# A second tile for the decay matrices in the scan of layer 2, paid for with one general tile

## The chip, the core and the metric

The kernel runs on one core of a Trainium2 chip. The time is that of the device, in microseconds (us), as the median of several executions: 2751.73 us over three (2747.14 to 2757.44). One further execution was profiled. All order, wait and idle times below are from that one.

The engines are TensorE (PE, with PEld for its weight loads), VectorE (DVE), ScalarE (ACT), GpSimd (POOL), and SyncE (SP), which issues the DMAs. Each takes its instructions strictly in the order in which they stand in its queue.

## What is computed

Two model blocks over 1024 tokens of width 1024, all in float32. The change lies in the second layer of the first block, a state-space layer (SSD): an input projection, a short convolution, a scan over chunks of 128 tokens, a gate with a norm, and an output projection. The scan, cut to what matters:

```
cs    = cumsum(dt * a_neg)                         # inside each chunk of 128
decay = where(causal, exp(cs[l] - cs[s]), 0)       # 128 x 128 per head and chunk
cb    = einsum('bclgn,bcsgn->bcgls', cc, bc)       # C times B, per group
y_diag = einsum('bcghls,bcsghp->bclghp', cb * decay, xf)
states = einsum('bclgn,bclghp->bcghpn', bc, xf * decay_states)
h      = h * chunk_decay + states                  # from chunk to chunk
y_off  = einsum('bclgn,bcghpn->bclghp', cc, prev) * exp(cs)
```

There are 32 heads of width 64 in 4 groups (8 heads share one B and C), and 8 chunks.

## The kernel before, in words

Every large product is made of three float32r products (helper `mm3`, lines 189, 193 and 194): each operand is split into a high part (a cast on ScalarE) and a low part (`lo`, line 260, a subtraction on VectorE or GpSimd).

The scan is in `phase_b`. It goes in 32 steps (u, cpair): u counts half groups (4 heads each), cpair pairs of chunks. Eight steps belong to one group. A step has two halves:

- `stage1` transposes x on TensorE (line 891, tile `t`), scales it on VectorE to `Xf` (L898), splits that into `Xh` (L902) and `Xl`; loads `L`, the cumulative sums of 4 heads and 2 chunks spread over 128 partitions, by DMA (L907); makes the decay of it on ScalarE (eight short L911, one exp L913), multiplies it by the masked C-B product `cbm` (L916), and splits it into `Lh` (L918) and `Ll` (L260). Then it adds to the running state: products `t<-Xh,bth`, `hs` on VectorE (L934 to L937), `hh` on ScalarE (L940), `hl`.
- `stage2` makes the output of the step: products of the state (`ch`, `hh`) and of the decay (`Lh`, `Xh`) into the PSUM tiles `u` and `w`, gathered in `et` on VectorE (L971, L974, L988), the gate `zt` (L991), a square on ScalarE (L997), and stores.

```
L = self.tag("L", "L")
nc.sync.dma_start(L..., csd[...].partition_broadcast(128))
...
Lh, Ll = R("Lh"), R("Ll")
nc.scalar.copy(Lh, L)
self.lo(nc.vector, Ll, L, Lh)
```

Beside the scan run the input projections of the groups still to come (PSUM tile `g`, two of them; 48 products of 128x512 each). A projection of x, B or C ends with `conv_silu`: `xb` and `xc` on ScalarE (L810, L812) read `g` and free it, four passes on VectorE follow (L815, L817), and a tanh (L816). One of z ends with L873 and L874. Which projections follow which step stands in `PATTERN`. In the last step of a group the next step's `stage1` waits until the new group's B and C are loaded, transposed and split (`load_bc`, `prep_bc`). After the last projection, `y_act` (L1071 to L1076, cast `XH` at L1075) prepares the first part of the output projection, in general tiles too.

`stage1` of step k+1 is written ahead of `stage2` of step k. Its tiles are: `L` from a tag of its own, whose number of buffers is in `TAGS`; `Xf`, `Xh`, `Xl`, `Lh`, `Ll`, `xb`, `xc`, `cbm`, `bc`, `yl` and others from the tag `P`, whose number is the first argument of `phase`. Both hold 128x1024 float32.

The order of the instructions on the engines is not the written one. A planner takes them by written order, as soon as by its own model of time their inputs and a free tile are there, and fixes the order on every engine before the program runs. A tile that comes free earlier thus moves instructions everywhere after it.

Of the kernel before, what the change touches and what calls it, by code (L numbers as in the profile page):

```python
# [21 lines left out]
ORDER = "c0 k0 q0 c1 q1 k1 r0 q2 c2 q3 k2 r1 q4 c3 q5 k3 r2 q6 g4 q7 r3 g0 g1 g2 g3 g5 v0 g6 g7"  # L22

PATTERN = "x x b zz b x x zz".split()
TAGS = dict(Z=1, L=1, S=4)
ALPHA = 2.0 ** 0.5
MLA_SCALE = 96.0 ** -0.5
SB_SCALE = 64.0 ** -0.5
# [21 lines left out]
class K:  # L50
# [52 lines left out]
    def tag(self, tag, nm, dt=F32):  # L103
        return self.ap.tile([128, T], dt, tag=tag, bufs=TAGS[tag], name=self.nm(nm))

# [1681 lines left out]
    def run(self, out):  # L1787
        with self.psum(g=2, t=2, u=1, w=1):
            with self.phase(18, 0, 3, 0, 3):
                self.phase_a()  # L1790
            with self.phase(10, 27, 0, 4, 3, "P"):
                self.attend_a()
            self.x2d = self.dp.tile([D, T], F32, name="x2d")
            with self.phase(17, 4, 0, 4, 2):
                self.phase_b()
                self.finish_b()
                self.project_c()
        with self.phase(9, 32, 0, 0, 3, "B"):
            with self.psum(s=3, t=3, u=1, f=1):
                self.attend_c()  # L1800
            with self.psum(m=8):
                self.mlp_up()
                t = self.mlp_down()
            with self.psum(m=4, t=3, u=1):
                self.mlp_last(t)
                self.phase_e(t, out)
# [120 lines left out]
```

## Time and profile before

| | us |
|---|---|
| median of three executions | 2751.73 |
| profiled execution | 2756.04 |
| its span | 2753.9 |
| TensorE busy | 2610.7 |
| VectorE busy | 1920.8 |
| ScalarE busy | 1453.5 |
| mean granted TensorE clock | 0.967 of full speed |

The span is what the profile covers; 2.1 us of the execution lie around it. Busy shares are averages over stages with different limits. The scan of layer 2 takes some 560 to 1260 us of the span. A timeline row reads: start, duration, engine, line, operation, tiles written and read, shape, count, and in brackets how long the engine stood idle before it and what ended that.

### The profile page before, as it was taken

Reading aid. Unit: us, or ns where it says so; the run is one execution under the profiler, and the core shown is the slowest. Engines: PE = TensorE matmul, PEld = TensorE weight load, DVE = VectorE, ACT = ScalarE, POOL = GpSimd, SP = SyncE. Lnnn points to the kernel's source line nnn. Section 1 sums busy time; section 2 is a strip of 40 time slices with the busy share of each in tenths; the row PEclk is TensorE's granted clock in tenths of the full one; section 3 lists DMA queues with packets and bytes.
Section 4 is the critical chain, followed back from the end, with each engine's and each line's share of the span. In section 5 each row is a group of like instructions: output and inputs, shape, how many; then the busy total and the mean of one; then the engine's idle time right before and its main releaser. Section 6 shows DMA issues by size and latency. Waiting matters only on the chain.

```text
span 2753.9 us, 34523 instructions
## 1 busy us (share of the span) xinstructions
PE 2610.7 (95%) x12000; PEld 2091.4 (76%) x12000; DVE 1920.8 (70%) x2806; ACT 1453.5 (53%) x2495; POOL 528.7 (19%) x383
## 2 busy tenths in 40 slices
PE   8999999999989999789999999999999999999998
PEld 6777887787877788677767776667688888887786
DVE  4683766779978698785585214888796667777576
ACT  5553754656655555543464224676665455343465
POOL 2642654400000000004455322333000000000000
PEclk9999999999999999889999998989999999999999
DMA  3444433443534334366433343543454446976324
GB/s 127 157 160 142 138 92 104 145 142 112 141 96 130 123 118 139 99 214 216 146 125 98 115 138 111 151 113 117 165 205 145 155 146 222 333 251 237 113 83 149
DMA packets 214419, 407.15 MB, mean 148 GB/s; under 512 B 22636, under 2 KB 61548, under 8 KB 214244
## 3 DMA queue, kind: packets, MB, share of 16 engines
q1 hardware_dynamic: 214244, 404.93, 45.6%
q8 instruction: 95, 1.56, 0.2%
q14 instruction: 80, 0.66, 0.1%
HBM read 297.35 MB, written 107.50 MB: 147 GB/s over the span
## 4 chain that ended last, share of the span: by engine, by line
PE 41%; DVE 4%; DMA 2%; ACT 2%; issue 2%; POOL 0%; DVEq 0%; SPq 0%; ACTq 0%; POOLq 0%
PE m L189 6%; PE m L193 6%; PE m L194 6%; PE g L194 2%; PE g L193 2%; PE g L189 2%; PE t L189 2%; PE t L194 2%; PE t L193 2%; DMA a<-w_down 2%; PE s L1274 1%; DVE XL L260 1%; PE t L574 1%; PE f L189 1%; PE f L193 1%
## 5 line engine op out<-in xcount | busy, mean ns | idle before, releaser
L189 PE MATMUL g<-XH,wh 128*128 128x512 f32 x1296 | 526.7, 407 | 22.5 <-ACT xc L812 9.4
L193 PE MATMUL g<-XL,wh 128*128 128x512 f32 x1296 | 524.7, 405 | 5.9 <-DVE XL L260 3.4
L194 PE MATMUL g<-XH,wl 128*128 128x512 f32 x1296 | 522.8, 404 | 4.1 <-POOL wl L260 4.1
L180 ACT CAST wh<-wr 128x512 fp32r<-128x512 f32 (+2 forms) x367 | 221.1, 604 | 416.2 <-PE g L193 166.9
L260 POOL TENSOR_TENSOR wl<-wr,wh 128x512 fp32r<-128x512 f32 (+2 forms) x198 | 280.1, 1418 | 415.9 <-ACT wh L180 378.7
L189 PEld LDWEIGHTS g<-XH,wh 128*128 128x128 f32 x1296 | 249.1, 192 | 84.2 <-ACT xc L812 10.6
L193 PEld LDWEIGHTS g<-XL,wh 128*128 128x128 f32 x1296 | 249.1, 192 | 68.3 <-DVE XL L260 7.1
L194 PEld LDWEIGHTS g<-XH,wl 128*128 128x128 f32 x1296 | 248.6, 192 | 64.0 <-POOL wl L260 5.2
L260 DVE TENSOR_TENSOR wl<-wr,wh 128x512 fp32r<-128x512 f32 (+1 forms) x262 | 183.9, 711 | 113.9 <-ACT wh L180 58.6
L1773 POOL TENSOR_TENSOR o<-t,rst 128x256 f32<-128x256 f32 x6 | 5.3, 912 | 824.6 <-ACT rst L294 824.6
L193 PE MATMUL m<-XL,XH 128*128 128x512 f32 x368 | 145.3, 395 | 5.8 <-DVE XL L260 5.8
L260 POOL TENSOR_TENSOR yl<-yl,yh 128x1024 fp32r<-128x1024 f32 x4 | 9.6, 2403 | 715.1 <-ACT yh L1075 712.3
L194 PE MATMUL m<-XH,XL 128*128 128x512 f32 x368 | 144.2, 392 | 0.0
L189 PE MATMUL m<-XH,XH 128*128 128x512 f32 x368 | 143.7, 392 | 0.0
L911 ACT ACTIVATE L<-L,tm 128x128 f32<-128x128 f32 x256 | 78.7, 389 | 122.3 <-DMA L<-csd 122.3
L189 PE MATMUL t<-XH,wh 128*128 128x512 f32 (+1 forms) x328 | 129.4, 394 | 0.6 <-ACT wh L180 0.6
L194 PE MATMUL t<-XH,wl 128*128 128x512 f32 (+1 forms) x328 | 128.8, 393 | 0.8 <-DVE wl L260 0.4
L193 PE MATMUL t<-XL,wh 128*128 128x512 f32 (+1 forms) x328 | 128.4, 392 | 0.0
L1613 ACT CAST XH<-a 128x1024 fp32r<-128x1024 f32 x46 | 48.3, 1049 | 138.3 <-PE m L193 115.0
L1281 POOL TENSOR_TENSOR sg<-sg,kp 128x127 f32<-128x127 f32 (+3 forms) x64 | 85.4, 1341 | 162.4 <-DVE kp L1280 116.3
L1280 DVE TENSOR_TENSOR_SCAN kp<-kp,zero 128x128 f32<-128x128 f32 (+3 forms) x64 | 96.1, 1509 | 22.3 <-ACT kp L1278 20.5
L577 ACT CAST XL<-t 128x256 fp32r<-128x256 f32 (+2 forms) x192 | 78.5, 430 | 45.0 <-PE t L574 22.7
(584 smaller groups left out, 6579.6 us busy)
## 6 DMA issues: line engine op xcount, KB each, us to landing
a<-w_down SPq DMA_DIRECT2D x64, 512.0 KB, 5.2
b<-hd SPq DMA_DIRECT2D x48, 512.0 KB, 5.1
wr<-wb_in SPq DMA_DIRECT2D x90, 256.0 KB, 2.8
wr<-wc_in SPq DMA_DIRECT2D x72, 256.0 KB, 2.9
L<-csd SPq DMA_DIRECT2D x32, 512.0 KB, 5.7
wr<-w_up SPq DMA_DIRECT2D x28, 512.0 KB, 3.7
wr<-wb_out SPq DMA_DIRECT2D x48, 256.0 KB, 4.9
hd<-t SPq DMA_DIRECT2D x48, 256.0 KB, 2.3
```

The source lines that it names most:

```text
L180: nc.scalar.copy(hi[:, :n], raw[:, :n])
L189: first = nc.tensor.matmul(ps, w[0], a[0], start=start, stop=False, skip_group_check=more)
L193: nc.tensor.matmul(ps, w[0], a[1], start=False, stop=False, skip_group_check=more)
L194: nc.tensor.matmul(ps, w[1], a[0], start=False, stop=stop, skip_group_check=more)
L260: eng.tensor_tensor(out, src, hi.bitcast(F32), op=A.subtract)
L574: nc.tensor.transpose(ps[:, c:c + 128], Pn[qi][:, (k0 + j) * 128:(k0 + j) * 128 + 128], self.ident)
L577: nc.scalar.copy(th[:, y], ps[:, x])
L911: nc.scalar.activation(Lv[:, c, h, :], Lv[:, c, h, :], AF.Relu, scale=-1.0, bias=cs_t[:, (c0 + c) * 32 + h0 + h:(c0 + c) * 32 + h0 + h + 1])
L1274: nc.tensor.matmul(ps, qst[a, qc], kl[a, c:e], start=False, stop=not last)
L1280: nc.vector.tensor_tensor_scan(rv, rv, zero.to_broadcast([128, W]), 1.0, op0=A.mult, op1=A.add)
L1281: nc.gpsimd.tensor_tensor(sg[:, :W - 1], sg[:, :W - 1], kp[:, 1:W], op=A.mult)
L1613: nc.scalar.copy(hi, x)
```

## The change

The tag `L` gets two buffers in place of one, and the phase of the scan has sixteen general tiles in place of seventeen. The memory is the same.

```
-TAGS = dict(Z=1, L=1, S=4)
+TAGS = dict(Z=1, L=2, S=4)
...
-            with self.phase(17, 4, 0, 4, 2):
+            with self.phase(16, 4, 0, 4, 2):
                 self.phase_b()
                 self.finish_b()
                 self.project_c()
```

No instruction is added or taken away; the planner places those of the scan differently. The first instruction that moves is on SP, the load of the second `L`, shortly before the first step of the scan.

**ScalarE at the second restart, first part** (the first step of the second group). Names: `Xh_1141`, `Lh_1144` and `L_1143` belong to the first step of the group, `L_1173` to its second, `L_1202` to its third; `acc2_940` holds the norm of the group before. Before:

```order
L902 CAST Xh_1141_6653<-Xf_1140_6648 128x1024
L291 ACT_TABLE_LOAD
L291 ACTIVATE acc2_940_5407<-u_1127_6584,eps_435 128x512
L918 CAST Lh_1144_6670<-L_1143_6657 128x1024
L294 ACT_TABLE_LOAD
L294 ACTIVATE acc2_940_5407<-acc2_940_5407 128x512
L180 CAST wh_1221_7093<-wr_1220_7092 128x512
L911 ACTIVATE L_1173_6838<-L_1173_6838,tm_4940 128x128 x8
```

Now:

```order
L902 CAST Xh_1141_6653<-Xf_1140_6648 128x1024
L918 CAST Lh_1144_6670<-L_1143_6657 128x1024
L291 ACT_TABLE_LOAD
L291 ACTIVATE acc2_940_5407<-u_1127_6584,eps_435 128x512
L180 CAST wh_1243_7245<-wr_1242_7244 128x512
L294 ACT_TABLE_LOAD
L294 ACTIVATE acc2_940_5407<-acc2_940_5407 128x512
L911 ACTIVATE L_1202_7002<-L_1202_7002,tm_4940 128x128 x8
```

`Lh` of the first step stands ahead of the logarithm of the old group's norm, and the `L` that follows is that of the third step in place of the second. On SP the load of this `L` moved from behind the store of that norm (L1009) to ahead of it.

**ScalarE at the second restart, further on.** `Lh_1174` belongs to the second step of the group, `L_1202` to the third, `L_1230` to the fourth; `wh_1271` is the high part of the weights of a projection to come, `hh_1178` and `hh_1181` are states, `g_1195` is the projection tile that `xb` and `xc` free. Before:

```order
L918 CAST Lh_1174_6851<-L_1173_6838 128x1024
L180 CAST wh_1246_7251<-wr_1245_7250 128x512
L940 CAST hh_1178_6862<-hs_1177_6859 128x256
L911 ACTIVATE L_1202_7002<-L_1202_7002,tm_4940 128x128 x8
L180 CAST wh_1271_7413<-wr_1270_7412 128x512
L913 ACTIVATE L_1202_7002<-L_1202_7002 128x1024
L940 CAST hh_1181_6872<-hs_1180_6869 128x256
L997 ACTIVATE et_1184_6883<-zt_1185_6888 128x512
L810 COPY xb_1196_6979<-g_1195_6930 128x1024
L812 ACTIVATE xc_1197_6981<-g_1195_6930,hw_4920 128x1024
```

Now:

```order
L918 CAST Lh_1174_6851<-L_1173_6838 128x1024
L940 CAST hh_1151_6690<-hs_1150_6687 128x256
L940 CAST hh_1178_6862<-hs_1177_6859 128x256
L180 CAST wh_1271_7413<-wr_1270_7412 128x512
L911 ACTIVATE L_1230_7170<-L_1230_7170,tm_4940 128x128 x8
L940 CAST hh_1181_6872<-hs_1180_6869 128x256
L913 ACTIVATE L_1230_7170<-L_1230_7170 128x1024
L997 ACTIVATE et_1184_6883<-zt_1185_6888 128x512
L810 COPY xb_1196_6979<-g_1195_6930 128x1024
L812 ACTIVATE xc_1197_6981<-g_1195_6930,hw_4920 128x1024
```

`wh_1271` moved from behind the `L` to ahead of it, and the `L` between `Lh_1174` and `xb_1196` is the next step's.

**TensorE at the third restart.** `t_1387` are the first transposes of the third group; `g_1443` and `g_1471` are the last two projections before the next that has to wait. Before:

```order
L189 MATMUL g_1443_8438<-XH4_68,wh_1441_8433 128x512
L193 MATMUL g_1443_8438<-XL4_76,wh_1441_8433 128x512
L891 MATMUL t_1387_8151<-ident_r_370,xc_1342_7875 128x128
L891 MATMUL t_1387_8151<-ident_r_370,xc_1369_8038 128x128
L891 MATMUL t_1387_8151<-ident_r_370,xc_1342_7875 128x128
L891 MATMUL t_1387_8151<-ident_r_370,xc_1369_8038 128x128
L194 MATMUL g_1443_8438<-XH4_68,wl_1442_8434 128x512
```

Now:

```order
L193 MATMUL g_1471_8606<-XL2_74,wh_1466_8595 128x512
L194 MATMUL g_1471_8606<-XH2_66,wl_1467_8596 128x512
L891 MATMUL t_1387_8151<-ident_r_370,xc_1342_7875 128x128
L891 MATMUL t_1387_8151<-ident_r_370,xc_1369_8038 128x128
L891 MATMUL t_1387_8151<-ident_r_370,xc_1342_7875 128x128
L891 MATMUL t_1387_8151<-ident_r_370,xc_1369_8038 128x128
L189 MATMUL g_1471_8606<-XH3_67,wh_1466_8595 128x512
```

The transposes moved from the middle of `g_1443` to the middle of the projection after it, 40 of the 128x512 products later. At the first and second restart they moved 17 and 22 of these products later, at the fourth 33 earlier.

## Rows read from the trace of the kernel before

**Rows 1.** The page, part 1: busy time, share of the span, instructions of each engine.
```profile
PE 2610.7 (95%) x12000; PEld 2091.4 (76%) x12000; DVE 1920.8 (70%) x2806; ACT 1453.5 (53%) x2495; POOL 528.7 (19%) x383
```

**Rows 2.** Stretches of 40 us: length, busy PE, PEld, DVE, ACT, POOL, PEclk, DMA, GB/s.
```profile
780.00:820.00 40.00, 31.79 (x148) 26.13 (x147) 33.10 (x61) 21.95 (x39) 0.00 (x0) 0.83 0.33 93
940.00:980.00 40.00, 31.59 (x149) 25.62 (x148) 29.75 (x60) 21.37 (x40) 0.00 (x0) 0.87 0.32 87
980.00:1020.00 40.00, 40.00 (x200) 33.30 (x199) 35.38 (x58) 25.40 (x48) 0.00 (x0) 1.00 0.41 128
1100.00:1140.00 40.00, 29.13 (x126) 24.38 (x125) 27.83 (x55) 24.15 (x40) 0.00 (x0) 0.74 0.28 83
1140.00:1180.00 40.00, 32.03 (x161) 27.52 (x159) 34.24 (x61) 19.38 (x36) 0.00 (x0) 0.84 0.52 140
```

**Rows 3.** Waits of TensorE from 500 to 1300: us in total, times, longest.
```profile
PE t L189 <- ACT Xh L902: 17.0, 8, 5.5
PE g L189 <- ACT xc L812: 9.4, 4, 3.4
PE w L189 <- DVE et L988: 6.3, 3, 5.3
```

**Rows 4.** Waits of ScalarE from 555 to 1290, the first.
```profile
ACT L L911 <- DMA L<-csd: 122.3, 29, 9.1
```

**Rows 5.** Timeline of TensorE: T and G of the four restarts.
```profile
607.15 0.60 PE L891 MATMUL t<-ident_r,xc 128*128 128x128 f32 x4
...
637.68 0.50 PE L189 MATMUL g<-XH,wh 128*128 128x512 f32 x1 [3.04 <-ACT xc L812]
...
759.49 0.38 PE L891 MATMUL t<-ident_r,xc 128*128 128x128 f32 x2
...
799.91 0.79 PE L189 MATMUL g<-XH,wh 128*128 128x512 f32 x1 [1.69 <-ACT xc L812]
...
931.23 0.44 PE L891 MATMUL t<-ident_r,xc 128*128 128x128 f32 x2
...
967.70 0.79 PE L189 MATMUL g<-XH,wh 128*128 128x512 f32 x1 [1.28 <-ACT xc L812]
...
1098.56 0.49 PE L891 MATMUL t<-ident_r,xc 128*128 128x128 f32 x3
...
1132.72 0.80 PE L189 MATMUL g<-XH,wh 128*128 128x512 f32 x1 [3.44 <-ACT xc L812]
```

**Rows 6.** Timeline of VectorE and ScalarE at the first restart.
```profile
611.46 1.22 DVE L260 TENSOR_TENSOR Ll<-L,Lh 128x1024 fp32r<-128x1024 f32 x1
...
617.72 2.45 ACT L911 ACTIVATE L<-L,tm 128x128 f32<-128x128 f32 x8 [3.90 <-DMA L<-csd]
...
631.41 2.45 ACT L911 ACTIVATE L<-L,tm 128x128 f32<-128x128 f32 x8 [3.34 <-DMA L<-csd]
```

**Rows 7.** Timeline of ScalarE at the second restart.
```profile
774.19 2.45 ACT L911 ACTIVATE L<-L,tm 128x128 f32<-128x128 f32 x8 [5.77 <-DMA L<-csd]
...
789.70 2.44 ACT L911 ACTIVATE L<-L,tm 128x128 f32<-128x128 f32 x8 [5.22 <-DMA L<-csd]
```

**Rows 8.** Timeline of TensorE at 759: projection products that follow each other.
```profile
759.02 0.40 PE L194 MATMUL g<-XH,wl 128*128 128x512 f32 x1
759.26 0.39 PE L189 MATMUL g<-XH,wh 128*128 128x512 f32 x1
```

**Rows 9.** Timeline of TensorE at 872 and 888.
```profile
872.17 0.38 PE L189 MATMUL t<-Xh,bth 128*128 128x256 f32 x1 [1.81 <-ACT Xh L902]
...
887.89 0.58 PE L189 MATMUL t<-Xh,bth 128*128 128x256 f32 x1 [2.32 <-ACT Xh L902]
```

**Rows 10.** Timeline of ScalarE at 1164.
```profile
1164.38 2.44 ACT L911 ACTIVATE L<-L,tm 128x128 f32<-128x128 f32 x8 [2.52 <-DMA L<-csd]
```

## The prediction

> **What bounds the kernel now.** I read the page's first part, then the scan of layer 2 by stretches, then who waits for whom there, and last the timeline at the places where TensorE stands still. The page shows TensorE busy for 95% of the span and no other engine over 70% [rows 1]. The change touches the scan alone (some 560 to 1260 us of the span), so only time lost there can be won. By stretches, the loss is not spread evenly. From 980 to 1020 TensorE is busy throughout at the full clock, but from 780, 940, 1100 and 1140 it is busy for 29 to 32 us of 40, at a mean granted clock of 0.74 to 0.87 of the full 2.4 GHz [rows 2]. These are the places where a new group of heads begins. The scan's chain has run empty there (the last step of a group starts no next one), and two steps must pass before the projections can go on. I call such a place a restart. There are four: the first at 607 us, then at 759, 931 and 1099.
>
> Who waits: in the scan TensorE stands mostly before its products with Xh, before projection products that wait for xc (the copy on ScalarE that frees their PSUM tile), and for et on VectorE: 17.0, 9.4 and 6.3 us [rows 3]. ScalarE in turn waited 122.3 us, in 29 of the 32 steps, for the DMA that brings L [rows 4]. ScalarE runs its queue in order, so whatever stands behind L there waits too.
>
> At each restart I take two moments: T, the first transposes (L891) of the new group, and G, the first projection product that had to wait for xc. From T to G it took 30.5, 40.4, 36.5 and 34.2 us [rows 5]. In the first restart the 30.5 us are three legs: 10.6 us from T to the first L that ScalarE waits for, 13.7 us to the next, 6.3 us from there to G [rows 5, 6]. In the second restart the legs are 14.7, 15.5 and 10.2 us [rows 5, 7]. Each of the first two legs is a load of L that may start only when Ll of an earlier step is done: at the first restart Ll ended at 612.68 and ScalarE began with the loaded L at 617.72, 5.0 us later [rows 6].
>
> **The change part by part.** No instruction is added or removed. L gets a second buffer, the general tiles lose one, and the planner places everything in the scan anew.
>
> *The second L buffer.* The load of L for step k now waits for Ll of step k-2, and not k-1. That looks as if the wait must vanish. But the new order on ScalarE puts L of step k+1 just as close behind Lh of step k-1 as L of step k stood before, and ahead of work that is needed sooner. At the second restart the L of the fourth step stands four instructions behind Lh of the second, with xb and xc of the projection behind it. So two loads of L stay in the way from T to G, and I take the three legs of the first restart as the price of all of them: 10.6 + 13.7 + 6.3 = 30.5, less about 0.5 since Lh no longer waits for its own L. What goes is the extra of the later restarts. In the second, the order now puts the wh that VectorE needed ahead of L, and not behind it, so its last leg loses the difference of 3.9 us; and Lh now stands ahead of the logarithm of the old group's norm, and the load of L on SP ahead of that norm's write, which takes the first leg from 14.7 to some 11 us. New T to G: 30, 30, 32 and 30 us (in the third, Xf came late on VectorE, which stays). Won: 0.5, 10.4, 4.5 and 4.2 us, 19.6 in all.
>
> *Where the restarts stand.* The order moves T among the projection products. Counted in the order from the G before, T comes 17, 22 and 40 of them later at the first three restarts and 33 earlier at the fourth; the number of other products ahead of T stays the same. A product takes 0.23 us [rows 8]. TensorE takes its queue in order, and what stands between a G and the next T keeps it busy, so T itself comes 4.0, 5.1 and 9.3 us later and 7.7 us earlier. The products that now run before T are missing behind it, where they filled the time from T to G. But that time is set by the chain: it holds 60 to 67 short products and the projections left over, by my estimate 15 to 25 us of work in 30. Net: +10.7 us.
>
> *Stalls between restarts.* The waits for Xh at 872 and 888 us (1.8 and 2.3) [rows 9] stood behind an L on ScalarE. In the new order the L of the first has more work ahead of it, and the product of the second stands some 2.6 us of products later on TensorE. I take both as gone: 4.1 us. Bounds: 0 and, with the clock that fell after them, some 6.
>
> *After the projections.* At 1164 ScalarE waited 2.5 us for L between the last z and Xh [rows 10]. Now the L there is one step younger and stands ahead of z, which has to wait for its product anyway. Won 2.5 us, at least 0 and at most 10, the whole gain of the second restart.
>
> *One general tile less.* The trace shows no wait for a free tile by name; it would appear as an xb, xc, Xf or yl that begins late. The nearest row is the 9.4 us for xc [rows 3]. One tile less could double that, and could also order it better and save it: -9.4 to +9.4. I take 0, since the four Gs hang on ScalarE's order and not on the tile. Behind the scan the order of TensorE is nearly the same, so nothing is counted there.
>
> Sum: first restart +4.0 - 0.5 = +3.5; second +5.1 - 10.4 = -5.3; third +9.3 - 4.5 - 4.1 = +0.7; fourth -7.7 - 4.2 = -11.9; after the projections -2.5. Total -15.5 us. The profiled execution took 2756.0 us (its span 2753.9), so 2740.5 by its own time. The median of the runs shown is 2751.7, 4.3 below it, and I set the forecast against that: 2736 us.
>
> The rows say that ScalarE's wait for L is set by where the order puts L, not by the number of buffers. The Trainium skill, "Trainium Kernel Development and Optimization", section "Best Practices", says to double-buffer so that DMA overlaps compute; by that rule the wait of 122 us would go and the third rival below would hold. By the row and the new order most of it stays.
>
> **Rivals.**
> *The gain is eaten, no change (2752).* If the later legs keep half of their extra (T to G 30, 35, 34 and 32, so 11 us won in place of 19.6) and the two stalls stay, what is won by the chain is paid by the +10.7 us of moved restarts: 2751.7 + 10.7 - 11 = 2751. For it: the legs at the first restart show that a load on the way costs 5.0 us after Ll however early the order means it. Against it: the second restart's last leg was lengthened by one wh, and that wh has moved.
>
> *Slower (2762 to 2770).* The wait for L on ScalarE keeps all four T to G as they were, and the place of T decides: +4.0 + 5.1 + 9.3 - 7.7 = +10.7, so 2762; and if the earlier T of the fourth restart is of no use, because VectorE, busy for 35.4 of 40 us between restarts [rows 2], can't bring its group forward by 7.7 us, +18.4, so 2770. It decides once T to G at the third restart is again over 36 us. For it: VectorE's share. Against it: between the third and fourth restart no wait on VectorE stands in the rows.
>
> *Much faster (about 2697).* The second buffer hides the loads: the waits of TensorE for Xh, xc and et go (17.0 + 9.4 + 6.3 = 32.7 us [rows 3]), and with them the low clock of the four stretches, (1 - clock) x busy: 5.4 + 4.1 + 7.6 + 5.1 = 22.2 us [rows 2]. Together 55 us. Against it: ScalarE's order, as above. Part of it, by 25 to 40 us, is likelier than the whole.
>
> **How the numbers follow.** Measured medians tell apart about 0.5%, 13.8 us: below 2738 counts as faster, above 2765.5 as slower. Forecast 0.47, with its own range of 2724 to 2748 (the bounds of the stalls and of the last term, and half of those of the tile); just over half of that lies below 2738: 0.27 faster, 0.20 same. No change 0.18, all same except what the tile costs more (0.03 slower). Slower 0.16: 0.11 slower, 0.05 same. Much faster, in part or whole, 0.19. Together: faster 0.46, same 0.40, slower 0.14. The range leaves out one in ten at each end: on the low side the larger part of the third rival, on the high side the upper end of the second: 2706 to 2764.
>
> **What would show it.** In the profile after: ScalarE still waits for L in most steps, 80 us or more in all (if under 30, the third rival holds). T to G is near 30 us at all four restarts, the second shortened most. T stands 9.3 us of work later at the third restart and 7.7 earlier at the fourth, so TensorE's idle time at the third is not less than before, and at the fourth it is halved. The waits for Xh at 872 and 888 have no successor. TensorE's granted clock still falls at restarts. Wrong would be: T to G still above 34 us at the second restart; new waits of TensorE for bc or Xh between restarts, which would be the lost tile; a longer way from the last projection to the first output product; or a difference that lies outside the scan.

## The result, and the profile after

The changed kernel takes 2767.73 us (median of seven executions, 2761.41 to 2773.41), the kernel before 2751.73 (seven, 2747.14 to 2757.44): 1.0060 times as long, with a 95% interval of 1.0044 to 1.0076. Run once more beside other kernels it came out at 1.0068 (1.0052 to 1.0084). The forecast was 2736 us with a range of 2706 to 2764; the change is slower, by some 16 us, and the time lies outside the range.

The profiled execution took 2766.79 us, its span is 2764.7. First the page's line of engines, that answers to [rows 1].

```profile
PE 2608.6 (94%) x12000; PEld 2091.1 (76%) x12000; DVE 1928.6 (70%) x2806; ACT 1454.4 (53%) x2495; POOL 538.5 (19%) x383
```

TensorE is as busy as before (2610.7 us) in a span that is 10.8 us longer. Two of the stretches of [rows 2], in the same columns:

```profile
940.00:980.00 40.00, 30.59 (x137) 25.52 (x135) 30.00 (x60) 23.47 (x40) 0.00 (x0) 0.74 0.27 76
...
1100.00:1140.00 40.00, 31.88 (x152) 25.56 (x151) 30.65 (x64) 24.20 (x42) 0.00 (x0) 0.87 0.30 99
```

The restarts are still there: 30.59 and 31.88 busy us of 40 here, the granted clock at 0.74 and 0.87. Now who waits from 500 to 1300 us (us in total, times, longest), to be laid beside [rows 3, 4].

```profile
ACT L L911 <- DMA L<-csd: 108.3, 30, 10.5
...
PE g L189 <- ACT xc L812: 10.3, 5, 3.3
...
PE w L189 <- ACT hh L940: 7.2, 3, 3.0
PE t L189 <- ACT Xh L902: 6.2, 5, 1.7
...
PE u L189 <- ACT hh L940: 4.7, 2, 2.8
```

ScalarE's wait for L went from 122.3 to 108.3 us only. TensorE waits 10.8 us less for Xh, but 11.9 us for hh, for which it had no wait before. T and G of the four restarts, as in [rows 5]:

```profile
609.42 0.60 PE L891 MATMUL t<-ident_r,xc 128*128 128x128 f32 x4
...
640.36 0.79 PE L189 MATMUL g<-XH,wh 128*128 128x512 f32 x1 [2.21 <-ACT xc L812]
...
771.34 0.60 PE L891 MATMUL t<-ident_r,xc 128*128 128x128 f32 x4
...
803.53 0.80 PE L189 MATMUL g<-XH,wh 128*128 128x512 f32 x1 [2.50 <-ACT xc L812]
...
941.13 0.60 PE L891 MATMUL t<-ident_r,xc 128*128 128x128 f32 x4
...
971.95 0.80 PE L189 MATMUL g<-XH,wh 128*128 128x512 f32 x1 [3.33 <-ACT xc L812]
...
1100.35 0.60 PE L891 MATMUL t<-ident_r,xc 128*128 128x128 f32 x4
...
1137.22 0.79 PE L189 MATMUL g<-XH,wh 128*128 128x512 f32 x1 [1.70 <-ACT xc L812]
```

T to G is 30.9, 32.2, 30.8 and 36.9 us, against 30.5, 40.4, 36.5 and 34.2 before.

To find where the time went, three stretches of TensorE's timeline are enough. Their ends are products that both kernels have: one just ahead of the first restart, the fourth G, a product of the last but one output tile, and the first sum product (L1147) of the next stage. Of before (without its G, [rows 5]):

```profile
599.10 0.40 PE L189 MATMUL g<-XH,wh 128*128 128x512 f32 x1
...
1268.81 0.39 PE L189 MATMUL g<-XH,wh 128*128 128x512 f32 x1
...
1470.97 0.39 PE L1147 MATMUL w<-sh,sels 128*40 128x512 f32 x1
```

And of after:

```profile
597.40 0.39 PE L189 MATMUL g<-XH,wh 128*128 128x512 f32 x1
...
1273.36 0.39 PE L189 MATMUL g<-XH,wh 128*128 128x512 f32 x1
...
1482.28 0.40 PE L1147 MATMUL w<-sh,sels 128*40 128x512 f32 x1
```

| stretch, us | before | after | after again | forecast of the difference |
|---|---|---|---|---|
| restarts: to the fourth G | 533.6 | 539.8 | 541.3 | -13.0 |
| last steps: to 1268.81 | 136.1 | 136.1 | 137.1 | -2.5 |
| end: to the next stage | 202.2 | 208.9 | 213.0 | 0 |

The first row ends with the fourth G, the second with the product that stands at 1268.81 before, the third with the next stage. So in these traces the restarts lost 6 to 8 us in place of winning 13, and the end, for which nothing was counted, lost 7 to 11. Kernels below that have the same order of the restarts tell how good one trace is: two with the order of before took 534.6 and 534.8 us there, one with the order of after 537.4. So one trace of this stretch is good to some 4 us, and the restarts lost 3 to 8.

The first row holds the same number of TensorE products in both kernels. TensorE's busy time in it, before and after, in the columns of [rows 2]:

```profile
599.10:1132.72 533.62, 494.84 (x2495) 411.90 (x2493) 440.12 (x787) 304.28 (x528) 0.00 (x0) 0.95 0.41 121
...
597.40:1137.22 539.82, 500.33 (x2496) 416.64 (x2494) 446.15 (x793) 305.65 (x528) 0.00 (x0) 0.94 0.41 119
```

Length less busy time is the time that TensorE stood: 38.8 us before, 39.5 after and 39.8 in the second trace. So the change took no idle time out of the restarts. The rest is products that ran longer, by 5.5 us (6.6 in the second trace), at a mean granted clock of 0.94 of full speed in place of 0.95. How the loss splits differs from one execution to the next: in the kernel of the 537.4 us, with the same order up to there, TensorE stood 41.7 us and was busy for 495.7.

### The profile page after: what moved, and what is told of

The parts are those of the page before. It is cut to its first block, busy times and chain, and to the rows that moved or that the text cites. A ratio compares the mean times of both kernels' runs of the same rounds, so it can differ in the third digit from the quotient of the medians.

```text
span 2764.7 us, 34500 instructions
## 1 busy us (share of the span) xinstructions
PE 2608.6 (94%) x12000; PEld 2091.1 (76%) x12000; DVE 1928.6 (70%) x2806; ACT 1454.4 (53%) x2495; POOL 538.5 (19%) x383
## 4 chain that ended last, share of the span: by engine, by line
PE 40%; DVE 5%; ACT 2%; DMA 2%; issue 1%; POOL 0%; DVEq 0%; SPq 0%; ACTq 0%
PE m L193 6%; PE m L189 6%; PE m L194 6%; PE t L194 2%; PE t L193 2%; PE t L189 2%; PE g L193 2%; PE g L189 2%; PE g L194 2%; DMA a<-w_down 1%; DVE XL L260 1%; PE s L1274 1%; PE t L574 1%; PE f L189 1%; DVE x L1120 1%
## 5 line engine op out<-in xcount | busy, mean ns | idle before, releaser
L911 ACT ACTIVATE L<-L,tm 128x128 f32<-128x128 f32 x256 | 78.7, 389 | 108.3 <-DMA L<-csd 108.3
L1281 POOL TENSOR_TENSOR sg<-sg,kp 128x127 f32<-128x127 f32 (+3 forms) x64 | 93.6, 1474 | 154.6 <-DVE kp L1280 136.7
L1280 DVE TENSOR_TENSOR_SCAN kp<-kp,zero 128x128 f32<-128x128 f32 (+3 forms) x64 | 96.5, 1527 | 12.8 <-ACT kp L1278 12.5
```

The lines of the kernel that those rows point to most:

```text
L911: nc.scalar.activation(Lv[:, c, h, :], Lv[:, c, h, :], AF.Relu, scale=-1.0, bias=cs_t[:, (c0 + c) * 32 + h0 + h:(c0 + c) * 32 + h0 + h + 1])
L1280: nc.vector.tensor_tensor_scan(rv, rv, zero.to_broadcast([128, W]), 1.0, op0=A.mult, op1=A.add)
L1281: nc.gpsimd.tensor_tensor(sg[:, :W - 1], sg[:, :W - 1], kp[:, 1:W], op=A.mult)
```

## Experiments

Theory A: the time follows from the order that the planner chose with two tiles for L, and from what stands behind a late L on ScalarE. Theory B: it is the lost general tile. In the kernels "held to an order" the program is planned twice: the first planning gives the order, and in the second every instruction on an engine is tied behind the one that the first put ahead of it.

**One tile less.** L keeps one tile.

```
-TAGS = dict(Z=1, L=2, S=4)
+TAGS = dict(Z=1, L=1, S=4)
```

> The kernel before with sixteen general tiles in place of seventeen and one tile for L, as before. Theory A (the time follows from the order that two tiles for L lead to): the lost tile alone moves little, 2744 to 2758 us, and ScalarE still waits some 120 us for L. Theory B (the lost general tile is what costs): most of the 16 us of the change are there with one L too, 2760 to 2772 us.

Measured: 2761.04 us, 1.0051 (1.0032 to 1.0070). Its restarts took 538.5 us, its end 208.2. Theory A's number missed: without the second tile for L, 14 of the 16 us are there. That is what B expects, but the order is a new one here too (T stands 18 and 19 products later than before at the second and third restart and 26 earlier at the fourth), so this run alone does not tell tile from order. What it does say: at sixteen general tiles the second L gave nothing that can be measured.

**L behind Lh.** The changed kernel with one more rule for the planner.

```
+                    if self.lh:
+                        self.tc.add_manual_dep(i.ins, self.lh, ...)   # i: the L911
...
-            nc.scalar.copy(Lh, L)
+            self.lh = nc.scalar.copy(Lh, L).ins.name
```

> The changed kernel, with the first eight instructions on L (L911) of a step held behind Lh of the step before in ScalarE's queue. Theory A (the second tile was spent on taking L one step earlier in ScalarE's queue; its load is still issued when Ll of two steps before ends, ScalarE waits 108 us for it, and hh, xc and Xh stand behind): the wait for L falls below 30 us, TensorE's waits of 2 to 3 us for hh at 710, 863, 955 and 1028 go, and the restarts get shorter: 2725 to 2745 us. Theory B (the lost tile): the tiles are as few as in the changed kernel, so 2757 to 2772 us.

Measured: 2724.81 us, 0.9910 (0.9879 to 0.9941): faster than both kernels, with as few tiles as the changed one. Its added lines move the line numbers up by one or more, L911 to L912 for one. ScalarE's whole wait for L from 555 to 1290 is one row:

```profile
ACT L L912 <- DMA L<-csd: 1.5, 1, 1.5
```

T and G of its fourth restart, now without a wait at G:

```profile
1075.06 0.60 PE L892 MATMUL t<-ident_r,xc 128*128 128x128 f32 x4
...
1101.57 0.79 PE L189 MATMUL g<-XH,wh 128*128 128x512 f32 x1
```

T to G is 27.7, 26.5, 28.6 and 26.5 us, the restarts together 502.7 in place of 539.8. TensorE stands 13.4 us of them. The second tile does hide the load, once L stands where it is needed and not a step ahead. This order differs elsewhere too (T stands 48 and 9 products later than before at the second and third restart), but no kernel here that has its loads and not this rule took less than 533 us for the restarts, and 502.7 is close to what the kernels without loads take, below.

**No load, in either order.** Both orders held on all engines, every load of L after the first (in the new order the first two) aimed at DRAM that nobody reads, each tile kept for good. `DROP` is false in the first planning and true in the second.

```
-            L = self.tag("L", "L")
+            L = stl[len(stl) - TAGS["L"]] if DROP and len(stl) >= TAGS["L"] else self.tag("L", "L")
...
+            dst = L if len(stl) < TAGS['L'] or not DROP else nol[u * 4 + cpair]
```

> Every engine is held to the order of the kernel before, but the loads of L after the first go to a place in DRAM that nobody reads, so no L waits for a load (the decay matrices hold old values; the amount of work is the same). Theory A (the load of L stands in the way at every restart, twice): 2752 less 25 to 45 us, 2707 to 2727. Theory C (what is ahead of or behind the load takes its place, VectorE above all): within 10 us of the kernel before, 2742 to 2752.

> The same with the order and the tiles of the changed kernel: every engine held to its order, the loads of L after the first two go where nobody reads. Theory A: 2768 less 30 to 50 us, 2718 to 2738, that is still about 10 us slower than the kernel before without its loads, since the loss behind the last projection (some 11 us by the two traces) has nothing to do with L. Theory B (waits for general tiles): above 2755, and TensorE's waits stay. If the whole difference of the change were in the loads, both kernels without loads would take the same time within 4 us.

Measured: 2713.85 us, 0.9878 (0.9858 to 0.9897), and 2717.67 us, 0.9897 (0.9876 to 0.9918). Theory C, as these expectations name it, fell: the load is worth 34 us in the order before (0.0122 of 2752). In the new order it is worth 45 (1.0060 less 0.9897), with two tiles. The restarts without loads, in the old order and in the new:

```profile
595.93:1093.10 497.17, 482.01 (x2495) 404.54 (x2493) 437.87 (x783) 307.83 (x527) 0.00 (x0) 0.98 0.47 129
...
594.96:1090.41 495.45, 481.65 (x2495) 404.13 (x2493) 444.28 (x793) 305.82 (x528) 0.00 (x0) 0.98 0.46 130
```

TensorE stands 15.2 and 13.8 us there. So the loads bring 24 us of idle time in the old order and 26 in the new: the second tile takes none of it away. The new order of the restarts is no worse by itself (495.5 us against 497.2); with the loads it loses more, 42 to 46 us over its three traces against 36 to 38, so 4 to 9 us.

The two medians differ by 3.8 us. That is within the 4 us that the expectation set for a difference that lies in the loads alone, but the traces show two parts that nearly cancel: without loads the new order is 4.1 us ahead at the product that stands at 1268.81 before, and loses 8.0 us from there to the end of the program. The loss at the end is there without the loads of L too: its stretch takes 202.0 us in the old order and 211.8 in the new.

**Five instructions ahead of L.** Order of the changed kernel held, but for five instructions of ScalarE.

```
+AHEAD = [("hh_1047", "L_1099"), ("hh_1260", "L_1318"), ("hh_1396", "L_1450"),
+         ("hh_1508", "L_1566"), ("wh_1766", "L_1726")]
```

> The changed kernel, every engine held to its order but for five instructions of ScalarE, which stand ahead of the L that they stood behind: hh ahead of L at 704, 859, 952 and 1025, and at the fourth restart wh ahead of L at 1127. Theory A (what stands behind a late L on ScalarE makes TensorE wait): its waits of 2.76, 2.30, 3.01 and 1.84 us for hh go, and the last leg of the fourth restart (10.6 us) gets some 3 us shorter: 12.8 us in all, 2768 to 2755, or 1.002 of the kernel before. Rival (other work is late there anyway): 2764 to 2771, 1.005 or more of the kernel before, and waits for something else stand in the same places.

Measured: 2761.43 us, 1.0047 (1.0032 to 1.0062). The sign is theory A's, the size is not: 4 to 6 us of 12.8 (against 1.0060 and 1.0068), and the interval meets those of the changed kernel, so a gain is not shown. The fourth restart went from 36.9 to 32.8 us, as expected. But where TensorE had waited for hh it now waits for the next link:

```profile
709.18 0.39 PE L192 MATMUL t<-Xh,bth 128*128 128x256 f32 x1 [1.30 <-ACT Xh L905]
...
860.60 0.33 PE L197 MATMUL w<-ch,hl 128*128 128x128 f32 x1 [1.04 <-DVE hl L263]
...
948.59 0.33 PE L197 MATMUL w<-ch,hl 128*128 128x128 f32 x1 [1.11 <-DVE hl L263]
```

**The last y tiles in L.** One line of `y_act`; up to the end of the scan the order is that of the changed kernel.

```
-        y = self.P("yl")
+        y = self.tag("L", "yl") if k > 7 else self.P("yl")
```

> The changed kernel, with the four last y tiles (the loads of finish_b, 128x1024) in the two L tiles, which are free by then, so that the end of the scan has its general tiles back. TensorE's order differs in some 30 places, all behind the last projection. Theory B for the end alone (the third of these loads waited for a free tile, at 1272 in place of 1263): the 9.8 us that were lost between the output products at 1273 and 1407 fall to 3 or less, so 2768 to about 2760, 1.003 of the kernel before. Rival (the end is late because the last steps are, or by the order of the weights): 2765 to 2770, 1.006.

Measured: 2757.13 us, 1.0034 (1.0020 to 1.0047). The end took 202.8 us, as in the kernel before. The last two of the four y loads, in the kernel before:

```profile
1263.35 0.39 SPq L1073 DMA_DIRECT2D yl<-yd  x1
1271.40 0.32 SPq L1073 DMA_DIRECT2D yl<-yd  x1
```

in the changed kernel, with what VectorE and TensorE did behind them (rows picked from the timelines):

```profile
1271.99 0.42 SPq L1073 DMA_DIRECT2D yl<-yd  x1
1276.84 1.29 DVE L1074 SCALAR_TENSOR_TENSOR yl<-yl,vec,rs 128x1024 f32<-128x1024 f32 x1 [5.25 <-DMA yl<-yd]
1279.77 0.68 DVE L971 TENSOR_TENSOR et<-et,w 128x512 f32<-128x512 f32 x1
1282.09 0.33 SPq L1073 DMA_DIRECT2D yl<-yd  x1
...
1293.75 2.05 PE L1007 MATMUL u<-acc,ones_r 128*128 128x512 f32 x2 [2.94 <-DVE acc L1002]
```

and with the y tiles in L:

```profile
1262.42 0.38 SPq L1073 DMA_DIRECT2D yl<-yd  x1
1264.40 0.63 SPq L1073 DMA_DIRECT2D yl<-yd  x1
```

VectorE stands in its queue 5.25 us for the third y and then 4.20 us for the fourth; the output of the last step (et) stands behind them, and the norm of the last group behind et. In L's tiles the loads come 7 and 15 us sooner, counted from the product that ends the second row of the table, and the 7 to 11 us at the end are gone.

**A tile kept back.** The kernel before, one general tile taken out of use behind the last step.

```
+        keep = self.P("keep")
+        i = nc.vector.memset(keep[:, 0:1], 0.0)
+        self.tc.add_manual_dep(i.ins, self.ll, ...)   # behind the last Ll
```

> The kernel before, seventeen general tiles and one L; behind Ll of the last step one general tile is taken out of use (one column of it is set on VectorE) and given back when finish_b is done. Up to there the order is that of before; behind it two products of TensorE, seven instructions of ScalarE and five of SP stand elsewhere. Theory B for the end alone: the third y load comes some 8 us later and the kernel is 5 to 10 us slower, 1.002 to 1.0035 of the kernel before. Rival (the end was late in the changed kernel for its order further up): 1.000, the third y load within 2 us of where it was.

Measured: 2751.81 us, 0.9998 (0.9986 to 1.0010). Theory B's time fell, though its first half came true: the third load was 6.3 us later, but the fourth was not.

```profile
1269.65 0.33 SPq L1073 DMA_DIRECT2D yl<-yd  x1
1271.21 0.32 SPq L1073 DMA_DIRECT2D yl<-yd  x1
```

The end took 204.9 us. So the tile missing at the end is not enough in the order of before. In the changed kernel the fourth load, at 1282.09, was let go when the store of the tile `t` landed that had been issued at 1279.28, and the VectorE instruction that makes this `t` stands behind the wait for the third y: one late load makes the next one late. That the order further up brings this about is argued and not tested.

**L written first, L written last.** The kernel before, its tiles untouched; in `stage1` the lines on L stand ahead of those on x, or behind those on the state.

```
+            L = self.tag("L", "L")   # with its 14 lines, moved up (or down)
             ps = self.t1()
```

> The kernel before with its own tiles (one L, seventeen general), the lines on L in stage1 written ahead of those on x: no work and no tile changes, the planner's order does. It asks how far an order alone moves the time. Theory of the order: it moves as far as the change did, by 5 us or more in either direction. If tiles are what counts: within 3 us of the kernel before, 0.999 to 1.001.

> The kernel before with its own tiles, the lines on L in stage1 written behind those on the running state. A second order with the same work and the same tiles, beside the one that came out 0.6% slower. If orders scatter: anywhere from 0.990 to 1.008. If the order before is one of the better ones of many: slower again, 1.003 or more. If tiles are what counts: 0.999 to 1.001.

Measured: 2761.54 us, 1.0058 (1.0040 to 1.0077), and 2751.57 us, 1.0005 (0.9987 to 1.0022). The second left the order of all engines in the scan as it was, and so is no second draw but a repeat. The first moved it, and lost as much as the change did, most of it at the restarts (544.9 us; the end took 201.8), with less waiting for L (76.1 us) and with other waits of TensorE in its place (11.3 us for et, 9.4 for the load of bc).

**The changed kernel again.**

> The changed kernel once more, beside the same runs of the kernel before: 1.0044 to 1.0076 as first measured. Its trace says how far a stretch differs from one execution to the next: the stretches between the anchors should agree within 2 us, and the end behind the last projection should again take some 10 us more than before.

Measured: 2771.86 us, 1.0068 (1.0052 to 1.0084). T to G were 30.8, 33.2, 31.0 and 37.1 us, each within 1.1 us of the first trace. The end came out 4.1 us apart (table above), more than the 2 us expected.

**Both small mends, both large ones.**

> The changed kernel with both small mends: the order of y_in_l held on every engine, but for the five instructions of ScalarE that stand ahead of the L that they stood behind. If the two parts of the loss are independent, the named parts add up: 1.0034 (y tiles in L) less the 0.0017 that the five instructions gave alone, 1.0015 to 1.002 of the kernel before, about 2755 us. If they overlap, 1.003 as with the y tiles alone. If the two explain the whole loss of the change, 1.000.

> Both mends at once: L911 of a step behind Lh of the step before, and the last y tiles in the L tiles. If the two are independent: 0.991 of the kernel before less the some 5 us that were lost behind the scan there, 0.988 to 0.990, about 2718 us. If the first already took what the second gives: 0.991.

Measured: 2754.22 us, 1.0027 (1.0006 to 1.0048), and 2722.46 us, 0.9915 (0.9897 to 0.9932). The first fits the sum (1.0015 to 1.002) as well as the y tiles alone; its restarts took 537.1 us, where the five instructions alone had 533.3 and the y tiles alone 537.4, so the 4 us of the five are not shown. The second is no better than L behind Lh alone.

## Why the prediction was wrong

**What held.** ScalarE still waits 108.3 us for L (forecast 80 or more). T to G came to 30.9, 32.2 and 30.8 us at the first three restarts (forecast 30, 30, 32), so the sizes were right. The reason is shown in part only. At the second restart the causes that the prediction names, 3.7 us in the first leg and 3.9 in the last, add up to 7.6 of its 10.4 us, and 8.2 were measured; and without any load these three ways are shorter in the new order too (24.4, 27.0 and 25.2 us against 27.5, 33.7 and 27.7). T's move in TensorE's queue was right at the first restart (G to T grew by 4.0 us, as forecast). The third restart came out as its sum had it, +0.6 against +0.7, in part by luck: G to T grew by 6.3 us (forecast 9.3 less 4.1), though TensorE's idle time there shrank by 2.0 only (4.3 to 2.3 us), with 2.30 us for hh at 863 in place of the stall at 872, and T to G by 5.7 (forecast 4.5).

**The step that failed at the restarts as a whole.** "But that time is set by the chain": by this step the work that moves ahead of T costs 10.7 us there and nothing is saved behind T, while the new order saves 19.6 us of the way from T to G and 4.1 us of stalls. Measured, the four ways from T to G became 10.8 us shorter and the ways from G to T 17.0 us longer (forecast 19.6 and 6.6). The projection products that left the ways from T to G (17 + 22 + 40 - 33, so 46) are 10.7 us of work at 0.23 us each. So what was won behind T is about what was moved ahead of it, and TensorE's idle time over all of it stayed at 39 to 42 us in the traces of either order, where the forecast needed it to fall by 13. Without loads it is 14 to 15 us, and with L behind Lh 13.4: the idle time was to be had from the load, and the second tile, in the planner's order, did not touch it. The longer run of the same products, 5.5 and 6.6 us in the two traces, had no term in the sum at all.

**After the projections: forecast -2.5, measured 0 and +1.0.** TensorE stood 5.47 us for Xh there before; in the two traces of the change it stood 4.35 and 3.86 us for et and then 1.23 and 0.69 for Xh. The stretch took 136.1 and 137.1 us against 136.1.

**The fourth restart: forecast -11.9, measured +0.3.** Two steps failed. T was to come 7.7 us earlier and came 2.5 earlier: between the third G and the fourth T, TensorE stood at 1028, 1042 and 1079 for 1.84, 1.69 and 1.00 us, where it had not stood before. And T to G was to become 30 and became 36.9. The 33 products that no longer stand ahead of T stand in it now: TensorE was busy for 28.8 us of it, and for 23.3 before, where the prediction had 15 to 25 us of work; without loads this way grew as well, from 27.0 to 30.3 us. TensorE still stands 8.1 us in it. The longest of its waits ends this chain, in rows picked from the timelines of SP, VectorE, ScalarE and TensorE of the changed kernel:

```profile
1120.39 1.22 DVE L260 TENSOR_TENSOR Ll<-L,Lh 128x1024 fp32r<-128x1024 f32 x1
1121.64 0.36 SPq L907 DMA_DIRECT2D L<-csd  x1
1126.67 2.45 ACT L911 ACTIVATE L<-L,tm 128x128 f32<-128x128 f32 x8 [2.45 <-DMA L<-csd]
1129.02 0.60 ACT L180 CAST wh<-wr 128x512 fp32r<-128x512 f32 x1
1129.65 0.69 DVE L260 TENSOR_TENSOR wl<-wr,wh 128x512 fp32r<-128x512 f32 x1 [2.87 <-ACT wh L180]
1130.60 0.84 DVE L988 TENSOR_TENSOR et<-et,w 64x256 f32<-64x256 f32 x2
1131.59 0.55 PE L189 MATMUL w<-Lh,Xh 128*128 128x256 f32 x1 [3.59 <-DVE et L988]
```

The load of the next L starts 0.03 us after the Ll that frees its tile, two steps back, and ScalarE stands for it with wh behind, VectorE for wh with et behind, TensorE for et. It is the very row that the forecast saw leave the second restart, one wh behind an L; the order had put it at the fourth, for which the prediction gives no order. With this wh ahead of L (five instructions ahead) the way took 32.8 us.

**The second restart: forecast -5.3, measured +0.9.** T to G won 8.2 of the 10.4. But G to T grew by 9.2 us and not by 5.1. One new wait in it is for an hh that had moved behind an L (rows picked from the timelines):

```profile
703.19 0.42 DVE L935 TENSOR_TENSOR hs<-hs,t 128x256 f32<-128x256 f32 x1
704.45 2.46 ACT L911 ACTIVATE L<-L,tm 128x128 f32<-128x128 f32 x8 [3.13 <-DMA L<-csd]
709.33 0.40 ACT L940 CAST hh<-hs 128x256 fp32r<-128x256 f32 x1
709.78 0.33 PE L189 MATMUL u<-ch,hh 128*128 128x128 f32 x1 [2.76 <-ACT hh L940]
```

hs was ready at 703.61, hh came at 709.33. The same stands at 863, 955 and 1028 (2.30, 3.01 and 1.84 us). But this wait is not the 4.1 us: from G to T TensorE stood 2.5 us in all before and 3.5 after, and with the hh ahead of L it still took 130.1 us in place of 131.0. The rest is 6 further short products, which stood ahead of the first G before, and a mean granted clock of 0.97 in place of 0.99 on this way; why the clock was lower is open. The forecast had named new waits for bc or Xh between restarts as what would make it wrong, as the mark of the lost tile. Most of the new ones were for hh, one of 1.69 us for Xh (at 1042), and the rows show a late L ahead of them on ScalarE and no missing tile.

**Behind the scan: forecast 0, measured 7 to 11 us.** "Behind the scan the order of TensorE is nearly the same, so nothing is counted there" is the step that failed most plainly. TensorE's order is nearly the same, but some instructions of SP, VectorE and ScalarE stand otherwise there, and the y loads need general tiles. The y tiles in L show that their tiles are part of it, the tile kept back that they are not all of it. "One general tile less", taken as 0 with bounds of 9.4 us to either side, thus missed in its place: its row was sought in the projections, and the tile was missed where no projection runs. Its bounds were narrow too: one tile less by itself, with the order that follows from it, lost 14 us (9 to 19 by its interval). A difference outside the scan was among the prediction's own signs of being wrong.

**The rivals.** The time, 2767.7, lies where the slower rival had it (2762 to 2770), but not by its mechanism: T to G did get shorter at the second and third restart, and what held back the fourth T was waits for ScalarE (hh, Xh and the norm), not VectorE. The much faster rival failed for the change. Its mechanism was right all the same, its price was not: with L behind Lh the wait goes, and the kernel is 25 us faster than before (0.0090), of the 55 that the rival had; against the changed kernel it is 41 us.

The Trainium skill, "Trainium Kernel Development and Optimization", section "Best Practices", asks for double buffers so that DMA overlaps compute. By the traces a second buffer alone took 14 of the 122 us of waiting (108.3 are left), and with L behind Lh nearly all (1.5 are left): only the second trace agrees with the rule.

## What to carry to other kernels

Here a second buffer gave time only where the consumer stayed in its place in the queue; a planner that takes a thing as soon as its own model allows spent the buffer on taking it sooner, and the engine waited as before, with other work behind. So when a buffer is added, look at what stands behind the wait on the waiting engine's queue, at every place and not at the worst one, and tie the consumer behind the work that does not need it. When work moves from one side of a mark to the other, add up the engine's idle time over both sides: one way gets shorter by what the other gets longer, and nothing is won. When a pool shrinks, look at every stretch that takes tiles from it (here the loss was at the end, where no projection runs). And before a difference of 0.5% is laid to a resource, make one order that differs with the resources equal: here that alone moved the time by 0.6%.

## What was not expected of the hardware

A stall of some 2 us does not always show in the clock. In the kernel before TensorE stood 2.35 us at 1301, and the granted clock from 1300 to 1320 was 1.00, the full 2.4 GHz:

```profile
1300.00:1320.00 20.00, 18.44 (x78) 14.68 (x79) 6.72 (x9) 6.00 (x10) 15.02 (x11) 1.00 0.73 234
```

With the tile kept back it stood twice there, 2.50 and 1.77 us, and the mean read 0.83, so the clock was at 1.2 GHz for a part of it:

```profile
1300.00:1320.00 20.00, 17.07 (x60) 13.35 (x61) 9.48 (x8) 5.87 (x10) 13.49 (x10) 0.83 0.64 204
```

From 1400 to 1500 it is the kernel before that has the lower clock (0.95 against 0.97). Counted from the product of 1268.81, the kernel with the tile kept back looked 6.2 us worse by 1392 and was 2.7 us worse by the next stage. A stretch that ends shortly behind a stall should be read on.

A subtraction of 128x512 on VectorE took 0.68 us in the scan, and up to 2.47 us beside one of GpSimd, as in the end of the changed kernel:

```profile
1268.63 2.40 POOL L260 TENSOR_TENSOR yl<-yl,yh 128x1024 fp32r<-128x1024 f32 x1 [5.25 <-ACT yh L1075]
1269.11 2.47 DVE L260 TENSOR_TENSOR wl<-wr,wh 128x512 fp32r<-128x512 f32 x1 [1.69 <-ACT wh L180]
```

GpSimd's ends at 1271.03, VectorE's at 1271.58: 0.55 us later, about the time that VectorE takes for one alone, as if it had waited for the other. In the kernel before two such subtractions, of 1.07 and 1.92 us at 1261.82 and 1268.09, end 0.55 us behind one of GpSimd as well. The Trainium skill, "SBUF — State Buffer", section "🎯 Summary: rules for kernel authors", says that when VectorE has two SBUF inputs while GpSimd's operation reads SBUF, the second of the two to issue blocks until the first is done; these rows agree.
